# Constant matmuls at the start, later gates, paired merges and two GpSimd splits in a hybrid recurrent and attention layer

## The chip, the cores and the metric

The kernel runs on one core of one Trainium2 chip. A time is the device time of one execution in microseconds (us). Five engines work side by side, each on its own queue of instructions in program order: TensorE (PE in the views, PEld for its weight loads), VectorE (DVE), ScalarE (ACT), GpSimd (POOL) and SyncE (SP, which here issues most of the DMA transfers). An engine waits at an instruction until what the instruction needs has been signalled, and everything behind it on that queue waits too.

## The reference, cut to what matters

One layer of a streaming encoder, for 512 rows of a prompt and 8 x 16 rows of samples (640 rows, 5 tiles of 128), width 1024:

```python
z = rmsnorm(x) @ w_in                      # u, gate, q, k, v
r = sigmoid(blockdiag(xc, wa) + ba); ig = sigmoid(blockdiag(xc, wi) + bi)   # xc = conv(u)
lru = scan(exp(-8 * r * softplus(-lam)), sqrt(1 - a * a) * ig * xc) * gelu(gate)
attn = sink_softmax(band(q, k)) @ v        # 8 heads of 64, own chunk and two before
h = x + concat(rmsnorm(lru), rmsnorm(attn)) @ w_out
q = rmsnorm(h) @ w_query                   # 8 heads, two halves of 128
top16 of q1 @ keys1 and of q2 @ keys2, top16 of the 256 sums   # 16384 experts
y = h + sum(softmax(top) * gelu(u[idx] . rmsnorm(h)) * v[idx])
```

## The kernel before, in words

Every f32 matmul of weight is made of three: both operands are split into a high part (a copy in the type fp32r) and a low part (what is left), and high x high, high x low and low x high are summed in PSUM. A weight comes in slabs of 128x2048 f32: SyncE loads `raw`, ScalarE writes the high part `wh` (L95), VectorE or GpSimd writes the low part `wl` (L100), as the argument of `next_slab` or `put` says; both have two buffers.

The order in which the lines are written is the order on each engine. The stages by the trace: the projection of k and v on one eighth of the depth after another (0 to 43 us, L182, with x split by ScalarE and VectorE as it arrives, L193 and L194, weights at L197 and L198, and sums of squares on GpSimd, L204); the projections U, Q and G with the attention of the prompt and the gates of the recurrent part between them (to 160 us); the merges (to 250 us); turning the rows and the query (to 396 us) with VectorE's top-16 on each half (`query_keys`, L907 to L912, to 409 us); then the experts, computed densely: a loop over 64 slabs of U (389 to about 1090 us, L948) and one over 64 slabs of V (to 1741 us, L1335). A step of the U loop is two blocks of 24 matmuls, and each block reads all of the step's slab.

PSUM has two pools: `bank()` gives one of four one-bank buffers (name pb), `wide()` one of two two-bank buffers (name pa). A buffer is given again, in turn, when what read it last is done.

`project(s, n, between)` (L429) runs eight steps of six matmuls and calls one of `between` after each step. `lru_gates` (L381) gives eight such calls: a matmul of 128x332 into a bank (L393) and a sigmoid on ScalarE that reads it (L394). Ahead of the second call of `project(G0, ...)` stand scores of the attention (L468, L469), whose exponentials on ScalarE (L485) read four banks.

A merge (L622 to L631) is 12 matmuls of 128x512 into a bank: one tile of rows, one half of the width, of the recurrent or of the attention part. VectorE then reads it in one instruction: L635 adds it to the rows of x, L643 writes the sum to `h_rows`. There are ten of each: in order (half 0, tiles 0 to 4), (half 1, tiles 0 to 4), twice. I number them 1 to 20. Between the first ones other work of the attention lies on TensorE (L502, L510, L534, L560, L576), and calls of `next_slab(V)` stand behind merges 1, 5, 10 and 15. From merge 8 to merge 20 they follow one another.

In the U loop (L1261 on) `put` at L1273 splits the slab of the next step. At c=1 and c=2 VectorE's queue still holds the top-16 of the last query half ahead of these splits.

Of the kernel before, what the change touches and what calls it, by code (L numbers as in the profile page):

```python
# [16 lines left out]
P = 128  # L17
# [31 lines left out]
def hybrid_layer(ctx: ExitStack, tc: tile.TileContext, i, o):  # L49
    nc = tc.nc  # L50
    V, A, G, PE = nc.vector, nc.scalar, nc.gpsimd, nc.tensor
# [14 lines left out]
    def wide():  # L66
        return pss.tile([P, 2, 512], F32, name="pa", tag="pa", bufs=2)

    def bank():
        return pss.tile([P, 512], F32, name="pb", tag="pb", bufs=4)  # L70
# [12 lines left out]
    ones = const.tile([P, P], F32, name="ones")  # L83
# [9 lines left out]
    def high(raw):  # L93
        wh = stream.tile([P, 2048], F32R, name="wh", tag="wh")
        A.activation(wh, raw, AF.Copy)  # L95
        return wh

    def low(raw, wh, eng):
        wl = stream.tile([P, 2048], F32R, name="wl", tag="wl")
        eng.tensor_sub(wl, raw, wh.bitcast(F32))  # L100
        return wl

    def kc(w, c=256):
        return [x.rearrange("p (k c) -> p k c", c=c) for x in w]

    def proj_T(ps, w, xh, xl, c, ks=range(KD)):

        wh, wl = w
        cs = slice(c * P, (c + 1) * P)
        for k in ks:  # L110
            for n, (a, b) in enumerate(((wh, xh), (wh, xl), (wl, xh))):
                for hf in range(2):
                    PE.matmul(ps[:, hf, :H2], a[:, k, cs], b[:, k, hf * H2:(hf + 1) * H2],
                              start=(k == 0 and n == 0), stop=(k == KD - 1 and n == 2))
# [41 lines left out]
    def parts_tile():  # L156
        return (sh.tile([P, KD, T], F32R, name="xh", tag="xh"),
                sh.tile([P, KD, T], F32R, name="xl", tag="xl"))
# [8 lines left out]
    for r in (0, 64):  # L167
# [2 lines left out]
        G.memset(mask_q[r + 32:r + 33, 64:128].bitcast(F32), 1.0)  # L170
        G.memset(mask_k[r + 32:r + 33, 0:64].bitcast(F32), FAR)
    xh, xl = parts_tile()
    rs1 = Rstd(wk, D)
    kv_ps = [wide(), wide()]
    kv_ps = [kv_ps[t // 2][:, t % 2, :256] for t in range(4)] + [bank()[:, :256]]
# [205 lines left out]
    def lru_gates(pair):  # L381

        r2 = wk.tile([P, 3, UL], F32, name="rg2", tag="kcT")
        q2 = wk.tile([P, UL], F32, name="q2", tag="vc")
        r1_ = wk.tile([P, 2, D], F32, name="rg1", tag="rg1").rearrange("p a b -> p (a b)")
        q1 = wk.tile([P, UL], F32, name="q", tag="t640", bufs=3)
        rg[pair[0]] = (*[r1_[:, n * UL:(n + 1) * UL] for n in range(3)], q1)
        rg[pair[1]] = (*[r2[:, n] for n in range(3)], q2)

        def gate(ct, n, hf):  # L390
            pg = bank()[:, :XL // 2]
            part = slice(hf * (XL // 2), (hf + 1) * (XL // 2))
            PE.matmul(pg, gates[n][:, ct, :], xcs[ct][:, part], start=True, stop=True)  # L393
            A.activation(rg[ct][n][:, part], pg, AF.Sigmoid,  # L394
                         bias=small[("lru_ba", "lru_bi")[n]][:, ct:ct + 1])

        return [lambda ct=ct, n=n, hf=hf: gate(ct, n, hf) for ct in pair for n in range(2) for hf in range(2)]
# [31 lines left out]
    def project(s, n, between=()):  # L429
        ps = wide()  # L430
        for k in range(KD):
            proj_T(ps, kc(slabs[s]), xh, xl, n, (k,))
            if k < len(between):
                between[k]()
        return ps
# [170 lines left out]
    def rsqrt(dst, v, ps, t, n):  # L606

        V.tensor_scalar(v[:, t], ps, 1.0 / n, EPS, op0=ALU.mult, op1=ALU.add)
        G.tensor_tensor(dst[:, t], v[:, t], mhalf[:, t], ALU.pow)
# [6 lines left out]
    def attn_sum(t, sq):  # L616
# [2 lines left out]
            PE.matmul(ps, sq[:, k], ones[:, 0:1], start=(k == 0), stop=(k == CT - 1))  # L619
        rsqrt(ra, rv_a, ps, slice(t, t + 1), LW)  # L620

    def merge(s, t, k0):  # L622

        ps = bank()
        wh, wl = kc(slabs[s], 512)
        ts_ = slice(t * P, (t + 1) * P)
        for n, (a, b) in enumerate(((ch, wh), (ch, wl), (cl, wh))):
            for k in range(CT):
                PE.matmul(ps, a[:, k0 + k, ts_], b[:, k, :], start=(k == 0 and n == 0),
                          stop=(k == CT - 1 and n == 2))  # L630
        return ps  # L631
# [14 lines left out]
    A01, A23 = (0, 1), (2, 3)  # L646
    U0, U1, Q1, G0, G1, L0, _, A0 = range(1, 9)
# [44 lines left out]
    pg = project(G0, 0)  # L692
# [6 lines left out]
    a, b, c, d = pr[1]  # L699
# [1 line left out]
    a.softmax()  # L701
    gate_rows(0, pg)
    a.divide()
    pg = project(G0, 1, lru_gates(A23))

    exchange(a, b)
    gate_rows(1, pg)
# [5 lines left out]
    pg = project(G1, 0)  # L713
# [13 lines left out]
    pg = project(G1, 1)  # L727
# [186 lines left out]
    U = {}  # L914

    def u_load(c):
        U[c] = [load_slab(i["u"][c]), None, None]

    def put(table, c, eng):
        table[c][1] = high(table[c][0])  # L920
        table[c][2] = low(table[c][0], table[c][1], eng)
# [5 lines left out]
    for u in range(2, 2 * PH):  # L927
        c, n = u // 2, u % 2
        if n == 0 and c + 1 == PH:
            u_load(0)  # L930
        ps = wide()
# [252 lines left out]
    NS = NK // 2  # L1184
# [3 lines left out]
    used, c = 0.0, 2  # L1188
# [9 lines left out]
    def own_work(c):  # L1198

        nonlocal first  # L1200
        if first is None:
            if "selected" in keep:
                first = c + 1
            return
        n0, n1 = [min(NO, NO * (x - first) // (2 * NS - 2 - first)) for x in (c, c + 1)]
        for n in sorted(rows):
            consume(n)
            if n == NR - 1:
                own_acts()
        for n in range(n0, n1):  # L1210
            fetch(n)

    Pv = {}

    def v_load(c):
        Pv[c] = [load_slab(i["v"][2 * c:2 * c + 2].rearrange("j p d -> p j d")), None, None]
# [4 lines left out]
    def group_piece(g, q):  # L1221

        if g >= NG:
            return
        if q == 0:
            (pg, tg_), (pa, ta_) = (((p2, "gt"), (p2, "at")), ((sh, "xh"), (sh, "xl")))[g % 2]
            ga[g] = (pg.tile([P, NCH, JG, TG], F32, name="gt", tag=tg_),
                     pa.tile([P, JG, SD], F32, name="at", tag=ta_))
        gt, at = ga[g]
        n = NCH // 4  # L1230
        nc.sync.dma_start(gt[:, q * n:(q + 1) * n], Gd[g][:, q * n:(q + 1) * n])
        nc.sync.dma_start(at[:, 2 * q:2 * q + 2], Ad[g][:, 2 * q:2 * q + 2, :])
# [3 lines left out]
    def weigh(c):  # L1236

        gt, at = ga[2 * c // JG]
        j0 = 2 * c % JG
        W[c] = at[:, j0:j0 + 2]  # L1240
        av = W[c].rearrange("p j (c t) -> p j c t", t=TG)
        V.tensor_mul(av, av, gt[:, :, j0:j0 + 2, :].rearrange("p c j t -> p j c t"))  # L1242

    def weigh_split(c):
        a2 = W[c]
        ph = p2.tile([P, 2, SD], F32R, name="ph", tag="ph", bufs=2)
        A.activation(ph, a2, AF.Copy)  # L1247
        pl = p2.tile([P, 2, SD], F32R, name="pl", tag="pl", bufs=2)
        V.tensor_sub(pl, a2, ph.bitcast(F32))  # L1249
        W[c] = (ph, pl)  # L1250
# [4 lines left out]
    def gelu_out(c, n):  # L1255
        A.activation(act[c][:, n], u_ps[c, n][:, :SD], AF.Gelu_apprx_tanh)  # L1256
        if n == 1:
            jj = 2 * c % JG
            nc.sync.dma_start(Ad[2 * c // JG][:, jj:jj + 2, :], act[c])

    for c in range(NS):  # L1261
        if c + 2 < NS:
            u_load(c + 2)
        else:
            v_load(c + 2 - NS)
        if c in (NS - 3, NS - 2):
            for q in range(2):
                group_piece(0, 2 * (c - NS + 3) + q)
        act[c] = ap_.tile([P, 2, SD], F32, name="act", tag="act")
        if pending:  # L1270
            gelu_out(*pending)
        if c:
            put(*((U, c + 1) if c + 1 < NS else (Pv, 0)), V)  # L1273
        if c == NS - 1:
            weigh(0)
        own_work(c)
        placing = [p for p in (plan[c - 1] if c else []) if p[4]]
        for n in range(2):
            if c or n:
                u_block(c, n)  # L1280
            if n == 0:
                for p in placing[:2]:
                    if p[3]:
                        p[3]()
                for p in placing[:2]:
                    if p[3]:
                        p[4]()
                gelu_out(c, 0)
                for p in placing[:2]:
                    if not p[3]:  # L1290
                        p[4]()
            else:
                for p in placing[2:]:
                    if p[3]:
                        p[3]()
                    p[4]()
                pending = (c, 1)
        for p in plan[c]:
            p[2]()
        for p in plan[c + 1]:  # L1300
            if p[1]:
                p[1]()
        if p2 is None and c > 1 and not any(plan[c - 1:]):
            close_tb()
            close_ta()
            p2 = ctx.enter_context(tc.tile_pool(name="p2", bufs=1))
        if c == NS - 1:
            weigh_split(0)
            gelu_out(*pending)
# [131 lines left out]
```

## Time and profile before

| | us |
|---|---|
| median of three runs | 1734.81 |
| lowest and highest | 1734.61, 1750.63 |
| the profiled execution | 1743.01 |
| its span | 1741.2 |
| TensorE busy in it | 1686.4 (97%) |
| VectorE busy | 1415.8 (81%) |
| ScalarE, GpSimd busy | 680.5, 680.9 (39%) |

All times below come from the profiled execution, from its span's start. In a timeline row the first number is when an instruction, or a run of equal ones (xcount), began, the second how long it lasted; out<-in are the names of the tiles; in brackets stands how long the engine was idle before it and what it waited for. Matmuls overlap: the distance between two starts tells more than a duration. PEclk in a windows row is the granted clock, 1.00 being the upper of the two levels.

### The profile page before, as it was taken

The page shows a single profiled execution, that of the slowest core. Times are in us where ns is not written, and L with a number is a line of the kernel's source. Part 1 is how long each engine was busy: PE and PEld are TensorE (multiplying, and loading weights), DVE is VectorE, ACT ScalarE, POOL GpSimd, SP SyncE. Part 2 cuts the span into 40 slices and gives each one's busy share as a digit, 9 for nine tenths or more (in the row PEclk, how much of TensorE's full clock was granted, in tenths as well). Part 3 has the DMA queues.
Part 4 walks back from the last instruction along what each step waited for, and adds up shares of the span by engine and source line. Part 5 has one row for each costly group of instructions (what it writes and reads, how often), then busy time and mean ns, then how long its engine had stood idle before and what let it go on. Part 6 is the DMA issues. An engine that isn't in the chain of part 4 may idle for free.

```text
span 1741.2 us, 24849 instructions
## 1 busy us (share of the span) xinstructions
PE 1686.4 (97%) x9634; PEld 1546.6 (89%) x9634; DVE 1415.8 (81%) x2350; ACT 680.5 (39%) x790; POOL 680.9 (39%) x483
## 2 busy tenths in 40 slices
PE   8989999999999999999999999999999899999998
PEld 7887789998999898989899898899999799999997
DVE  7766565997667999988998895788888788888887
ACT  5457333223444445454455552332232223232222
POOL 4122003230101444443444444455555455555452
PEclk9999999999999999999999999999999999999999
DMA  5213233123546898999899999999999899999995
GB/s 167 101 50 109 75 103 94 69 73 139 207 180 211 303 389 282 370 346 351 301 377 370 374 379 398 396 376 377 378 390 378 339 381 388 379 371 392 380 351 221
DMA packets 180983, 492.67 MB, mean 283 GB/s; under 512 B 16817, under 2 KB 75057, under 8 KB 170225
## 3 DMA queue, kind: packets, MB, share of 16 engines
q1 hardware_dynamic: 125424, 289.73, 46.5%
q0 software_dynamic: 55296, 201.35, 30.2%
q8 instruction: 75, 1.23, 0.3%
q14 instruction: 44, 0.35, 0.1%
q10 hardware_dynamic: 144, 0.00, 0.0%
HBM read 426.11 MB, written 65.48 MB: 282 GB/s over the span
## 4 chain that ended last, share of the span: by engine, by line
DVE 30%; PE 19%; DMA 12%; issue 10%; ACT 4%; POOL 1%; ACTq 0%; DVEq 0%; POOLq 0%; SPq 0%
PE pa L948 13%; DVE wl L100 10%; DVE h_rows L1172 9%; DMA raw<-in_u 7%; PE po L1335 5%; DVE at L1242 3%; ACT ph L1247 3%; DVE h_rows L1167 2%; DVE ring L1167 2%; DMA raw<-in_v 2%; DMA gt<-Gd 2%; ACT wh L95 1%; PE pb L1122 1%; DVE oh L1110 1%; DMA Gd<-stage 1%
## 5 line engine op out<-in xcount | busy, mean ns | idle before, releaser
L100 DVE TENSOR_TENSOR wl<-raw,wh 128x2048 fp32r<-128x2048 f32 x137 | 313.2, 2287 | 107.2 <-ACT wh L95 104.0
L1335 PE MATMUL po<-ph,wh 128*128 128x448 f32 x1024 | 376.3, 367 | 11.3 <-ACT ph L1247 5.8
L948 PE MATMUL pa<-xh,wl 128*128 128x448 f32 x1024 | 375.3, 366 | 5.9 <-DVE wl L100 5.9
L1335 PE MATMUL po<-pl,wh 128*128 128x448 f32 x1024 | 377.4, 369 | 2.3 <-DVE pl L1249 2.2
L948 PE MATMUL pa<-xh,wh 128*128 128x448 f32 x1024 | 378.1, 369 | 0.0
L1335 PE MATMUL po<-ph,wl 128*128 128x448 f32 x1024 | 375.7, 367 | 0.0
L948 PE MATMUL pa<-xl,wh 128*128 128x448 f32 x1024 | 374.5, 366 | 0.0
L95 ACT ACTIVATE wh<-raw 128x2048 fp32r<-128x2048 f32 x146 | 279.5, 1915 | 192.9 <-PE po L1335 101.5
L1160 POOL DMA_INDIRECT h_rows<-in_u_rows,rowi x96 | 142.8, 1487 | 330.6 <-DVE h_rows L1167 239.1
L1335 PEld LDWEIGHTS po<-ph,wh 128*128 128x128 f32 x1024 | 193.4, 189 | 28.0 <-ACT ph L1247 6.2
L1335 PEld LDWEIGHTS po<-pl,wh 128*128 128x128 f32 x1024 | 193.3, 189 | 24.4 <-DVE pl L1249 7.8
L948 PEld LDWEIGHTS pa<-xh,wl 128*128 128x128 f32 x1024 | 192.9, 188 | 22.6 <-DVE wl L100 7.3
L1335 PEld LDWEIGHTS po<-ph,wl 128*128 128x128 f32 x1024 | 193.3, 189 | 15.5
L948 PEld LDWEIGHTS pa<-xl,wh 128*128 128x128 f32 x1024 | 193.1, 189 | 14.7
L948 PEld LDWEIGHTS pa<-xh,wh 128*128 128x128 f32 x1024 | 193.1, 189 | 14.7 <-ACT act L1256 0.2
L1160 POOL DMA_INDIRECT h_rows<-in_v,rowi x96 | 147.6, 1538 | 144.0 <-DVE h_rows L1172 121.0
L1160 POOL DMA_INDIRECT ring<-in_u_rows,rowi x96 | 142.4, 1484 | 143.7 <-DVE ring L1167 120.3
L1160 POOL DMA_INDIRECT ring<-in_v,rowi x96 | 148.2, 1544 | 121.4 <-DVE h_rows L1172 100.1
L1247 ACT ACTIVATE ph<-at 128x896 fp32r<-128x896 f32 x64 | 61.0, 953 | 339.4 <-DVE at L1242 339.4
L1256 ACT ACTIVATE act<-pa 128x448 f32<-128x448 f32 x128 | 71.6, 559 | 238.7 <-PE pa L948 169.3
L1130 ACT ACTIVATE stage<-pb 128x512 f32<-128x512 f32 x112 | 109.7, 1131 | 58.3 <-PE pb L1122 58.1
L1249 DVE TENSOR_TENSOR pl<-at,ph 128x896 fp32r<-128x896 f32 x64 | 69.9, 1092 | 73.0 <-ACT ph L1247 71.9
(270 smaller groups left out, 2483.7 us busy)
## 6 DMA issues: line engine op xcount, KB each, us to landing
raw<-in_u SPq DMA_DIRECT2D x64, 1024.0 KB
raw<-in_v SPq DMA_DIRECT2D x64, 1024.0 KB
Ad<-act SPq DMA_DIRECT2D x64, 448.0 KB
Gd<-stage SPq DMA_DIRECT2D x28, 1024.0 KB
gt<-Gd SPq DMA_DIRECT2D x64, 448.0 KB
at<-Ad SPq DMA_DIRECT2D x64, 448.0 KB
raw<-in_w_query SPq DMA_DIRECT2D x8, 1024.0 KB
raw<-in_w_out SPq DMA_DIRECT2D x4, 1024.0 KB
```

What stands on the lines that cost most here:

```text
L95: A.activation(wh, raw, AF.Copy)
L100: eng.tensor_sub(wl, raw, wh.bitcast(F32))
L948: PE.matmul(u_ps[c, n][:, :SD], a[:, k, n * P:(n + 1) * P], b[:, k, :SD], start=(k == 0 and m == 0), stop=(k == KD - 1 and m == 2))
L1130: A.activation(d["stage"][:, :, t0:t0 + 4].rearrange("p j t -> p t j"), d[n, f], AF.Copy, scale=1.0 / GSC)
L1160: G.indirect_dma_start(out=rows[n], out_offset=None, in_=table, in_offset=bass.IndirectOffsetOnAxis(ap=rowi[:, c:c + 1], axis=0))
L1167: V.scalar_tensor_tensor(row, row, 1.0, xrow[:, n // NS_], op0=ALU.mult, op1=ALU.mult, accum_out=dots[:, n:n + 1])
L1172: V.scalar_tensor_tensor(y, row, slots[:, c:c + 1], y, op0=ALU.mult, op1=ALU.add)
L1242: V.tensor_mul(av, av, gt[:, :, j0:j0 + 2, :].rearrange("p c j t -> p j c t"))
L1247: A.activation(ph, a2, AF.Copy)
L1249: V.tensor_sub(pl, a2, ph.bitcast(F32))
L1256: A.activation(act[c][:, n], u_ps[c, n][:, :SD], AF.Gelu_apprx_tanh)
L1335: PE.matmul(po[k][:, :SD], a[:, j, k * P:(k + 1) * P], b[:, j, :], start=(c == 0 and j == 0 and n == 0), stop=(c == NS - 1 and j == 1 and ...
```

## The change

It has four parts. Ten matmuls of the constant `ones` with itself go into a bank of their own at the start of TensorE's queue. The eight gates that lie between the steps of the second `project(G0, ...)` come three steps later, the last three behind the projection. A merge takes its bank from a two-bank buffer of `wide()`, which two merges in a row share. And the low parts of the slabs 2 and 3 of U are made by GpSimd.

```diff
--- before.py
+++ after.py
@@ -170,6 +170,10 @@
         G.memset(mask_q[r + 32:r + 33, 64:128].bitcast(F32), 1.0)
         G.memset(mask_k[r + 32:r + 33, 0:64].bitcast(F32), FAR)
     xh, xl = parts_tile()
+
+    idle_ps = bank()
+    for _ in range(10):
+        PE.matmul(idle_ps[:, :P], ones, ones, start=True, stop=True)
     rs1 = Rstd(wk, D)
     kv_ps = [wide(), wide()]
     kv_ps = [kv_ps[t // 2][:, t % 2, :256] for t in range(4)] + [bank()[:, :256]]
@@ -619,9 +623,14 @@
             PE.matmul(ps, sq[:, k], ones[:, 0:1], start=(k == 0), stop=(k == CT - 1))
         rsqrt(ra, rv_a, ps, slice(t, t + 1), LW)
 
+    merge_ps = []
+
     def merge(s, t, k0):
 
-        ps = bank()
+        if not merge_ps:
+            two_banks = wide()
+            merge_ps.extend([two_banks[:, 1], two_banks[:, 0]])
+        ps = merge_ps.pop()
         wh, wl = kc(slabs[s], 512)
         ts_ = slice(t * P, (t + 1) * P)
         for n, (a, b) in enumerate(((ch, wh), (ch, wl), (cl, wh))):
@@ -701,7 +710,10 @@
     a.softmax()
     gate_rows(0, pg)
     a.divide()
-    pg = project(G0, 1, lru_gates(A23))
+    late = lru_gates(A23)
+    pg = project(G0, 1, [lambda: None] * 3 + late[:5])
+    for gate in late[5:]:
+        gate()
 
     exchange(a, b)
     gate_rows(1, pg)
@@ -1270,7 +1282,7 @@
         if pending:
             gelu_out(*pending)
         if c:
-            put(*((U, c + 1) if c + 1 < NS else (Pv, 0)), V)
+            put(*((U, c + 1) if c + 1 < NS else (Pv, 0)), G if c <= 2 else V)
         if c == NS - 1:
             weigh(0)
         own_work(c)
```

The rows of the order that follow are instructions in program order on one engine: the line, the operation, out<-in, the shape and, in brackets, the signals that this instruction waits for (DVE is VectorE's, Activation ScalarE's, PE TensorE's own). Lines of the changed kernel are 4 to 12 higher: L397 is the gate (L393 before), L638 the merge (L629 before).

First, TensorE in the second `project(G0, ...)`. Before, from its first step:

```order
L113 MATMUL pa<-xh,wh 128x320 x2
L113 MATMUL pa<-xl,wh 128x320 x2
L113 MATMUL pa<-xh,wl 128x320 x2
L393 MATMUL pb<-xc,wa 128x332 [waits PE_49]
L113 MATMUL pa<-xh,wh 128x320 x2
L113 MATMUL pa<-xl,wh 128x320 x2
L113 MATMUL pa<-xh,wl 128x320 x2
L393 MATMUL pb<-xc,wa 128x332 [waits Activation_49]
```

In the change, the end of the third step on:

```order
L113 MATMUL pa<-xh,wh 128x320 x2
L113 MATMUL pa<-xl,wh 128x320 x2
L113 MATMUL pa<-xh,wl 128x320 x2
L113 MATMUL pa<-xh,wh 128x320 x2
L113 MATMUL pa<-xl,wh 128x320 x2
L113 MATMUL pa<-xh,wl 128x320 x2
L397 MATMUL pb<-xc,wa 128x332 [waits PE_49]
L113 MATMUL pa<-xh,wh 128x320 x2
L113 MATMUL pa<-xl,wh 128x320 x2
L113 MATMUL pa<-xh,wl 128x320 x2
L397 MATMUL pb<-xc,wa 128x332 [waits Activation_49]
```

The first gate stands behind the fourth step, and its waits are as before: the third and the fourth wait for VectorE and ScalarE, which read the scores' banks.

Second, TensorE at merges 10 to 12. Before:

```order
L629 MATMUL pb<-wh,xh 128x512 [waits DVE_49]
L629 MATMUL pb<-wh,xh 128x512 x3
L629 MATMUL pb<-wl,xh 128x512 x4
L629 MATMUL pb<-wh,xl 128x512 x4
L629 MATMUL pb<-wh,xh 128x512 [waits DVE_49,Activation_49]
L629 MATMUL pb<-wh,xh 128x512 [waits Activation_49] x3
L629 MATMUL pb<-wl,xh 128x512 x4
L629 MATMUL pb<-wh,xl 128x512 x4
L629 MATMUL pb<-wh,xh 128x512 [waits DVE_49]
L629 MATMUL pb<-wh,xh 128x512 x3
L629 MATMUL pb<-wl,xh 128x512 x4
L629 MATMUL pb<-wh,xl 128x512 x4
```

In the change, from merge 10 (its first row has the wait) over merge 11 (its `x4` wait only for ScalarE, which makes their input) to merge 12:

```order
L638 MATMUL pa<-wh,xh 128x512 [waits DVE_49]
L638 MATMUL pa<-wh,xh 128x512 x3
L638 MATMUL pa<-wl,xh 128x512 x4
L638 MATMUL pa<-wh,xl 128x512 x4
L638 MATMUL pa<-wh,xh 128x512 [waits Activation_49] x4
L638 MATMUL pa<-wl,xh 128x512 x4
L638 MATMUL pa<-wh,xl 128x512 x4
L638 MATMUL pa<-wh,xh 128x512 [waits DVE_49]
L638 MATMUL pa<-wh,xh 128x512 x3
L638 MATMUL pa<-wl,xh 128x512 x4
L638 MATMUL pa<-wh,xl 128x512 x4
```

Before, the wait of merge 12 is for VectorE's read of merge 8, whose bank it takes over. In the change it is for VectorE's read (L652, which is L643 before) of merge 11, the first half of the same buffer. All second merges of a pair (2, 4, 6 and so on to 20) have such a wait, each for VectorE's read (L644 or L652) of the merge right before; the first ones have none for it.

Third, GpSimd's queue at the start of the U loop. Before:

```order
L958 IOTA first_of 128x128
L961 IOTA column 128x256
L964 IOTA io_4053 128x256
L1160 DMA h_rows<-in_u_rows,rowi 128x1024 [waits DVE_49]
L1160 DMA h_rows<-in_u_rows,rowi 128x1024
```

In the change:

```order
L970 IOTA first_of 128x128
L973 IOTA column 128x256
L976 IOTA io_4054 128x256
L100 TENSOR_TENSOR wl<-raw,wh 128x2048 [waits DMAHW4_49,PE_49,Activation_49]
L100 TENSOR_TENSOR wl<-raw,wh 128x2048 [waits DMAHW5_49,PE_49,Activation_49]
L1172 DMA h_rows<-in_u_rows,rowi 128x1024 [waits DVE_49]
```

Two splits (L100) stand between the last iota and the first gather (L1172, which is L1160 before). Nothing else moved on this queue, and VectorE's has two splits less.

## Rows read from the trace of the kernel before

**Rows 1.** Profile page, part 1: engine, busy us (share of the span) x instructions

```profile
PE 1686.4 (97%) x9634; PEld 1546.6 (89%) x9634; DVE 1415.8 (81%) x2350; ACT 680.5 (39%) x790; POOL 680.9 (39%) x483
```

**Rows 2.** Waits of TensorE, whole span: line, line waited for, us, times, longest

```profile
PE pb L1122 <- DVE ow L1114: 9.7, 7, 2.1
```

**Rows 3.** Timeline of TensorE, start; columns: start us, us, instruction, idle before

```profile
5.90 0.58 PE L182 MATMUL pa<-wh,xh 128*128 128x256 f32 x1 [5.90 <-ACT wh L197]
...
18.41 0.39 PE L182 MATMUL pa<-wl,xh 128*128 128x256 f32 x1 [1.56 <-DVE wl L198]
```

**Rows 4.** Timeline of VectorE, same stretch

```profile
1.41 0.17 DVE L84 MEMSET ones<- 128x128 f32 x1
...
5.93 0.69 DVE L198 TENSOR_TENSOR wl<-raw,wh 128x512 fp32r<-128x512 f32 x1
...
10.14 2.04 DVE L198 TENSOR_TENSOR wl<-raw,wh 128x512 fp32r<-128x512 f32 x1
```

**Rows 5.** Timeline of GpSimd, same stretch

```profile
9.83 3.78 POOL L204 TENSOR_TENSOR sq<-sq 128x640 f32<-128x640 f32 x2 [0.29 <-ACT sq L202]
```

**Rows 6.** Timeline of TensorE, second gate projection

```profile
118.96 0.56 PE L113 MATMUL pa<-xh,wh 128*128 128x320 f32 x2
...
119.95 0.72 PE L393 MATMUL pb<-xc,wa 128*128 128x332 f32 x2
...
121.39 0.72 PE L393 MATMUL pb<-xc,wa 128*128 128x332 f32 x2
...
126.61 0.83 PE L393 MATMUL pb<-xc,wi 128*128 128x332 f32 x2 [3.62 <-ACT p L485]
...
136.05 0.60 PE L502 MATMUL pb<-ident,p 128*128 128x128 f32 x4
```

**Rows 7.** Windows: busy us of PE, PEld, DVE, ACT, POOL; granted clock; DMA share; GB/s

```profile
128.00:129.00 1.00, 1.00 (x5) 1.00 (x4) 0.13 (x1) 0.99 (x3) 0.00 (x0) 0.50 0.00 0
179.00:181.00 2.00, 2.00 (x6) 1.53 (x5) 0.00 (x0) 2.00 (x9) 0.77 (x1) 0.50 0.00 0
```

**Rows 8.** Timeline of TensorE, merges

```profile
178.57 1.98 PE L629 MATMUL pb<-wh,xh 128*128 128x512 f32 x4 [1.33 <-DVE rv L136]
...
183.03 1.04 PE L502 MATMUL pb<-ident,p 128*128 128x128 f32 x8
...
204.38 1.17 PE L629 MATMUL pb<-wh,xh 128*128 128x512 f32 x4
...
220.64 1.07 PE L629 MATMUL pb<-wh,xh 128*128 128x512 f32 x4
...
226.08 1.07 PE L629 MATMUL pb<-wh,xh 128*128 128x512 f32 x4
```

**Rows 9.** Timeline of VectorE, same stretch

```profile
184.27 1.41 DVE L635 SCALAR_TENSOR_TENSOR rows<-pb,rr,rows 128x512 f32<-128x512 f32 x2
...
207.94 0.74 DVE L635 SCALAR_TENSOR_TENSOR rows<-pb,rr,rows 128x512 f32<-128x512 f32 x1
...
220.84 0.75 DVE L635 SCALAR_TENSOR_TENSOR rows<-pb,rr,rows 128x512 f32<-128x512 f32 x1 [0.92 <-PE pb L629]
...
227.72 0.75 DVE L643 SCALAR_TENSOR_TENSOR h_rows<-pb,ra,rows 128x512 f32<-128x512 f32 x1
```

**Rows 10.** Timeline of TensorE, second step of the U loop

```profile
411.36 0.74 PE L948 MATMUL pa<-xh,wl 128*128 128x448 f32 x1 [4.31 <-DVE wl L100]
...
414.59 0.36 PE L948 MATMUL pa<-xh,wl 128*128 128x448 f32 x1
...
415.81 0.36 PE L948 MATMUL pa<-xh,wl 128*128 128x448 f32 x1
```

**Rows 11.** Timeline of ScalarE, same stretch

```profile
397.40 1.91 ACT L95 ACTIVATE wh<-raw 128x2048 fp32r<-128x2048 f32 x1
...
407.12 1.90 ACT L95 ACTIVATE wh<-raw 128x2048 fp32r<-128x2048 f32 x1
```

**Rows 12.** Instructions of line 100: count, duration ns min/median/max, first and last start

```profile
L100 POOL TENSOR_TENSOR wl<-raw,wh x9: 4613/4628/4649, 265.3 to 388.1; 128x2048 fp32r<-128x2048 f32 x9
```

## The prediction

> **What bounds the kernel now.** I read the page first: TensorE is busy for 97% of the span [rows 1], so a change moves the time only by what it takes out of, or puts into, TensorE's row of work. Then the waits of TensorE over the whole span: the largest group is 9.7 us in seven pieces in the late loops [rows 2], which no edit touches; what the edits touch lies in four short places ahead of 412 us. For these I read the timeline of TensorE to see when it stands, then that of the engine it stands for. The reader is to see the idle time in brackets at the right end of a row: 5.90 and 1.56 us at the start [rows 3], 3.62 us at the third gate [rows 6], 1.33 us at the second merge [rows 8], 4.31 us at the split of slab 2 of U [rows 10]. [...]
>
> Behind 412 us nothing moves against its neighbours: every loop step is issued behind the one before, and TensorE is the engine with least slack. So I pass each shift of TensorE on to the end whole.
>
> **The change, part by part.**
>
> *Matmuls on constants.* Ten 128x128 products of a constant in f32. The smallest rows of that size are eight transposes in 1.04 us, 0.13 each [rows 8]; such an f32 product shows as two instructions in this trace, so 20 x 0.13 = 2.6 us, or 5.2 us at the low clock. They wait for the memset of the ones, done at 1.58 [rows 4], and end at 4.2 or at 6.8, against a first projection matmul at 5.90 [rows 3]. What they may bring is a faster projection. But that projection stands still again until 18.41 for VectorE's low part of a weight piece [rows 3], and VectorE's chain there waits for loads, ScalarE and itself, not for TensorE. So a quicker start only lengthens the 1.56 us stand, and a start 0.9 us late only shortens it. Upper end of the gain: nothing excludes that a few tenths pass; upper end of the loss: one fall of the clock at 18.41, where the stand is longer, 1.7 us by the price worked out under the merges. I take **0**.
>
> *Gates three steps later.* One step and its gate take 1.44 us (119.95 to 121.39), a step alone 0.99 at most (118.96 to 119.95) [rows 6]. The third gate is ready at 126.61 - 3.62 = 122.99 and stands for a PSUM bank that ScalarE's exponentials still read. Three plain steps ahead of it make it ready at 125.6 to 126.0; the exponentials do not depend on it, so 0.6 to 1.0 us of the stand is left and 2.6 to 3.0 go. From 119.95 to 136.05 are 16.1 us; less seven rounds of 1.44, a last gate of some 0.5 and the stand, 1.9 us is left, which is what the clock at 0.50 costs [rows 6, 7]. A stand of 1 us should not bring that fall: TensorE's 0.2 to 0.3 us are given back where the last three gates, now back to back, follow ScalarE's sigmoids. Gain 2.6 + 1.9 - 0.2 = **4.3 us**; 2.4 if the clock falls all the same.
>
> *Merges in pairs in a two-bank tile.* This is the term that decides. The twenty merges are each 2.72 us of TensorE (220.64 to 226.08 is two) [rows 8] and stood in banks of a ring of four, so that a merge rarely met VectorE. Now two merges share one tile. In the order of the change (the second place shown) the first matmul of every second merge carries a wait for VectorE, and the program fulfils it with VectorE's read of the first half of the same tile: the dependence is kept by tile, not by bank. So the second merge of a pair cannot start while the first is being read. What is late is read off VectorE's rows:
> - Merge 2: the read of merge 1 stands behind a slab split and starts at 184.27; two reads take 1.41, one 0.70. Start 184.97 instead of 178.57 [rows 8, 9]: +6.4 (the 1.33 us stand is inside it).
> - Merge 4: attention work lies between the halves: 0. Merge 8, in the same way: +0.1.
> - Merge 6: the read of merge 5 is behind a split too, 207.94 + 0.74 = 208.68 against 204.38: +4.3.
> - Merge 12: 227.72 + 0.75 = 228.47 against 226.08: +2.4.
> - Merges 10, 14, 16, 18, 20: back to back with their first halves. Read at 220.84 for 0.75, so 221.59 against 220.64 [rows 8, 9]: +0.95 each, 4.8.
>
> Sum 18.0. Behind each waiting merge all of TensorE's queue stands, and VectorE, which reads each merge as soon as it can, has no backlog in which the delay could vanish. Merge 2 ran at the low clock and took 183.03 - 178.57 = 4.46 instead of 2.72 [rows 7, 8]: a fall costs a merge 1.7. It stays at that price; merge 6 now follows 4.3 us of idle, as the matmuls after 4.31 us of idle in the U loop and after 3.62 us at the gate did when the clock fell, so +1.7. Together **+19.7**. Lower bound: 0 (the halves independent). Upper bound: a fall at every wait, six more, 10.4.
>
> [...] The row first: the stands that brought 0.50 are the long ones, or the 1.33 us one after light work. [...]
>
> *Two splits of U on GpSimd.* Before, both stand behind VectorE's top-k and TensorE gets slab 2 at 411.36, 4.31 us late, then runs at the low clock: 9 matmuls in 3.23 us, where six take 1.22 right after [rows 10], so 3.23 - 1.83 = 1.4 lost. On GpSimd a split takes 4.63 (nine of them, 4.61 to 4.65) [rows 12]. ScalarE's high part of slab 2 is there at 397.40 + 1.91 = 399.3 [rows 11]: ready at 403.9, needed at 411.36 - 4.31 = 407.05. Slab 3: 407.12 + 1.90 + 4.63 = 413.7, needed a step of 48 matmuls after slab 2, 48 x 0.203 = 9.7 us, at 416.8. GpSimd has nothing else then. Gain 4.3 + 1.4 = **5.7**. Moved past: only the gathers come behind these splits on GpSimd's queue, and those wait for indices that VectorE works out after its top-k. VectorE is rid of two splits while it is late. Lower bound: the third rival.
>
> **Sum**: 0 - 4.3 + 19.7 - 5.7 = +9.7 us. The profiled execution took 1743.01, so 1752.7 on its terms; it lies 8.2 over the median shown, 1734.81, and against that median I forecast **1744.5**, 0.56% slower. A measurement of this kernel tells about 1% from no change: 17.3 us, so 1717.5 to 1752.2 counts as the same.
>
> **Rivals.**
> 1. *The halves are independent*: the edit gives each merge a bank, and no more. Then the merge term is 0 to -1.3 and the others stay: -10.0 to -11.3, **1724**. For it: the two halves are different banks. [...] Against it: the wait in the order. It decides whether a second merge starts before VectorE's first read. 5%.
> 2. *The clock falls at the short waits too*: up to 6 x 1.74 = 10.4 more, **1755**, slower by more than 1%; it takes five of six falls. For it: merge 2's stand of 1.33 us was enough. Against it: the stands between are 0.95 us, and merges keep TensorE full in between. 10%. Merge 12 alone would give 1746.
> 3. *GpSimd's splits are stretched by VectorE.* VectorE's own subtract went from 0.69 to 2.04 us beside GpSimd's adds [rows 4, 5]. Three times 4.63 is 13.9: slab 2 at 413.2, 6.1 late, and slab 3 some 4 more, so +4 to +6 in place of -5.7: **1755**. It decides when a split passes 7.7 us (407.05 - 399.3). Against it: nine splits beside the same top-k at 4.61 to 4.65. 3%.
> 4. *Later waits swallow part of it*: the late loops wait for VectorE and loads at 9.7 us in all, and work that runs ahead of TensorE could be earlier by the shift: **1736**. Against it: those waits are in the step of the loops, not in an absolute time. 6%.
>
> My forecast keeps 76%. Its own bounds: 1738 (no fall at merge 6, a quicker start, a little less per wait) to 1750 (gates still at the low clock, a loss at the start, merge 12 at the low clock). With rival 4 and most of rival 2 the range is **1735 to 1754**. Faster by over 1%: 2%, slower by over 1%: 12% (rivals 2 and 3), within: 86%.
>
> **What would show it.** In the changed profile TensorE's first merge matmuls must show waits for VectorE's reads of merge results, ten at most, some 18 us in all beside the clock, longest at merges 2 and 6; the gate's wait near 1 us and no 0.50 at 128; no stand at 407 for the split; the projection at the start still going on at 18.4. I would be wrong if second merges start with no wait, if the clock shows 0.50 through the later merges, or if the GpSimd splits take over 7 us.

## The result and the profile after

The changed kernel took 1753.32 us (median of 21 runs, 1748.08 to 1756.63), the kernel before 1739.6 (21 runs, 1730.24 to 1750.63; the 1734.81 of the forecast was the median of its first three). The ratio is 1.0077, 95% interval 1.0062 to 1.0091: 13.4 us slower, 10.8 to 15.8. The forecast was 9.7 us slower on the median then known, with 1735 to 1754 as its range: the time lies inside it, near its upper end, and in the class it gave 86%, within 1%. Laid on 1739.6 instead, the same range would be 1740 to 1759.

The waits of TensorE in the changed kernel's profile, over the whole span (us in total, times, longest):

```profile
PE pa L638 <- DVE rows L644: 12.5, 3, 7.5
PE pa L638 <- DVE h_rows L652: 5.9, 5, 2.3
PE po L1347 <- ACT act L1268: 5.2, 1, 5.2
PE pb L1134 <- DVE ow L1126: 4.4, 5, 2.1
...
PE pb L397 <- ACT p L489: 1.0, 1, 1.0
```

The first two rows are new: eight stands of a merge for VectorE's read of a merge, 18.4 us. No row for a slab split (L100) is left, and the gate's wait is 1.0 instead of 3.62 [rows 6].

The timeline of TensorE at the merges, with the first transposes of the rows (L836) behind merge 20:

```profile
162.75 0.50 PE L638 MATMUL pa<-wh,xh 128*128 128x512 f32 x1 [1.59 <-ACT xh L752]
...
181.45 2.08 PE L638 MATMUL pa<-wh,xh 128*128 128x512 f32 x4 [7.53 <-DVE rows L644]
...
186.44 1.03 PE L506 MATMUL pb<-ident,p 128*128 128x128 f32 x8
...
212.13 1.20 PE L638 MATMUL pa<-wh,xh 128*128 128x512 f32 x4 [4.11 <-DVE rows L644]
...
221.02 2.07 PE L638 MATMUL pa<-wh,xh 128*128 128x512 f32 x4
...
232.69 1.20 PE L638 MATMUL pa<-wh,xh 128*128 128x512 f32 x4 [0.84 <-DVE rows L644]
...
240.73 2.07 PE L638 MATMUL pa<-wh,xh 128*128 128x512 f32 x4 [2.28 <-DVE h_rows L652]
...
245.14 1.09 PE L638 MATMUL pa<-wh,xh 128*128 128x512 f32 x4
...
271.74 1.91 PE L836 MATMUL pb<-ident,xn 128*128 128x128 f32 x16
```

These are merges 1, 2, 6, 7, 10, 12 and 13; they answer to [rows 8]. In the kernel before, merge 1 and the first transposes are these rows:

```profile
166.36 0.50 PE L629 MATMUL pb<-wh,xh 128*128 128x512 f32 x1 [1.59 <-ACT xh L740]
...
250.57 1.91 PE L824 MATMUL pb<-ident,xn 128*128 128x128 f32 x16
```

Merge 1 starts 3.6 us earlier than before, the transposes 21.17 us later: 24.8 us were lost between. VectorE, at the reads those stands were for:

```profile
178.44 2.29 DVE L100 TENSOR_TENSOR wl<-raw,wh 128x2048 fp32r<-128x2048 f32 x1 [3.54 <-ACT wh L95]
180.65 0.74 DVE L644 SCALAR_TENSOR_TENSOR rows<-pa,rr,rows 128x512 f32<-128x512 f32 x1
...
211.33 0.74 DVE L644 SCALAR_TENSOR_TENSOR rows<-pa,rr,rows 128x512 f32<-128x512 f32 x1
...
239.93 0.74 DVE L652 SCALAR_TENSOR_TENSOR h_rows<-pa,ra,rows 128x512 f32<-128x512 f32 x1
```

Read a row of one against the other: the read ends at 181.39 and merge 2 starts at 181.45; 212.07 and 212.13; 240.67 and 240.73. Each time 0.06 us lie between. And the windows (columns as in [rows 7]):

```profile
129.00:131.00 2.00, 2.00 (x11) 1.63 (x10) 0.00 (x0) 1.78 (x4) 0.07 (x1) 1.00 0.00 0
182.00:185.00 3.00, 3.00 (x8) 2.31 (x7) 0.00 (x0) 0.00 (x0) 0.00 (x0) 0.50 0.86 333
214.00:216.00 2.00, 2.00 (x7) 1.48 (x5) 0.00 (x0) 0.00 (x0) 0.00 (x0) 0.50 0.77 324
222.00:224.00 2.00, 2.00 (x7) 1.58 (x6) 1.05 (x3) 1.65 (x3) 0.00 (x0) 0.60 0.82 275
241.00:243.00 2.00, 2.00 (x5) 1.54 (x6) 0.00 (x0) 0.00 (x0) 0.00 (x0) 0.50 0.89 283
256.00:258.00 2.00, 2.00 (x10) 1.65 (x9) 1.28 (x1) 0.69 (x1) 0.00 (x0) 1.00 0.00 0
```

No 0.50 at the gates any more; 0.50 at merges 2, 6, 7 and 12 (0.60 is the end of that of merge 7); 1.00 at merge 16, which stood for 1.01 us. The clock is also at 0.50 at merges 1 and 5 (167 to 170 and 204 to 206 us), as in the kernel before (0.50 from 169 to 170 and from 200 to 202).

### The profile page after: what moved, and what is told of

It reads as the page before. It is cut to its first block, busy times and chain, and to the rows that moved or that the text cites. A ratio compares the mean times of both kernels' runs of the same rounds, so it can differ in the third digit from the quotient of the medians.

```text
span 1751.6 us, 24885 instructions
## 1 busy us (share of the span) xinstructions
PE 1695.5 (97%) x9654; PEld 1551.0 (89%) x9654; DVE 1415.8 (81%) x2348; ACT 680.1 (39%) x790; POOL 683.4 (39%) x485
## 4 chain that ended last, share of the span: by engine, by line
PE 46%; DVE 31%; DMA 8%; issue 8%; ACT 6%; POOL 0%; ACTq 0%; DVEq 0%; SPq 0%
PE pa L960 22%; DVE wl L100 9%; DVE h_rows L1184 9%; PE pa L113 8%; PE po L1347 5%; PE pa L638 3%; DVE at L1254 3%; ACT ph L1259 3%; DMA raw<-in_u 2%; DVE ring L1179 2%; DMA raw<-in_v 2%; PE pb L1134 2%; DMA gt<-Gd 2%; DVE h_rows L1179 2%; PE pb L186 1%
## 5 line engine op out<-in xcount | busy, mean ns | idle before, releaser
L100 DVE TENSOR_TENSOR wl<-raw,wh 128x2048 fp32r<-128x2048 f32 x135 | 308.7, 2286 | 98.1 <-ACT wh L95 94.9
L1172 POOL DMA_INDIRECT h_rows<-in_u_rows,rowi x96 | 142.3, 1482 | 303.8 <-DVE h_rows L1179 236.8
L1172 POOL DMA_INDIRECT h_rows<-in_v,rowi x96 | 147.6, 1537 | 144.1 <-DVE h_rows L1184 121.1
L1172 POOL DMA_INDIRECT ring<-in_v,rowi x96 | 148.1, 1543 | 121.6 <-DVE h_rows L1184 100.3
L1172 POOL DMA_INDIRECT ring<-in_u_rows,rowi x96 | 136.6, 1423 | 147.3 <-DVE ring L1179 124.2
```

The costliest lines, as they stand in the source:

```text
L1172: G.indirect_dma_start(out=rows[n], out_offset=None, in_=table, in_offset=bass.IndirectOffsetOnAxis(ap=rowi[:, c:c + 1], axis=0))
```

## The experiments

Ten more kernels ran, each timed in 5 to 12 executions beside 11 to 29 of the kernel before. The table has what was measured; the us are the ratio's, on the median of the kernel before beside it; "transposes" is the start of the first transposes of the rows in the run's profile.

| run | ratio to before (95%) | us against before | transposes, us |
|---|---|---|---|
| the change | 1.0077 (1.0062, 1.0091) | +13.4 | 271.74 |
| x1_bank_merges | 0.9924 (0.9902, 0.9946) | -13.2 | 248.97 |
| x2_merges_only | 1.0138 (1.0114, 1.0163) | +24.0 | 276.90 |
| x3_alternate | 0.9932 (0.9908, 0.9955) | -11.8 | 247.28 |
| x4_gates_splits | 0.9933 (0.9908, 0.9957) | -11.6 | 249.23 |
| x5_warm_only | 0.9999 (0.9983, 1.0015) | -0.2 | 253.10 |
| x6_gates_only | 0.9972 (0.9958, 0.9986) | -4.9 | 247.82 |
| x7_splits_only | 0.9954 (0.9936, 0.9971) | -8.0 | 252.09 |
| x10_read_first | 1.0002 (0.9987, 1.0016) | +0.3 | 257.52 |
| x11_alt_read_first | 0.9933 (0.9911, 0.9954) | -11.7 | 245.31 |
| x12_bank_read_first | 0.9937 (0.9910, 0.9963) | -11.0 | 249.32 |

**x1_bank_merges**, the change less the pairs:

```diff
-        if not merge_ps:
-            two_banks = wide()
-            merge_ps.extend([two_banks[:, 1], two_banks[:, 0]])
-        ps = merge_ps.pop()
+        ps = bank()
```

> The change with one part undone: merges take one-bank buffers again. Theory (the dependence is kept by two-bank tile, so every second merge waits for VectorE's read of the first): no wait of a merge for the read of the merge before it, the first transposes of the rows (250.57 us in the kernel before, 271.74 in the change) at 246.3 to 247.0, none of the clock's falls at merges 6, 7 and 12, and a time 9 to 10 us below the kernel before. Rival (the loss sits in another part: the constant matmuls, the gates or the GpSimd splits): the transposes stay behind 255 us, or the time stays above the kernel before.

One part taken out turns +13.4 into -13.2 us (-17.0 to -9.4; 9 to 10 were expected). No merge waits for the read before it; the one stand of merge 2 is the old one, for L136 (1.33 us). The transposes came 2 us later than the theory said: single merge matmuls took up to 0.80 us there against a median of 0.39, as in the kernel before, where the clock is at 0.50 at merges 1, 2 and 5, and those stretches differ from run to run (see the last section). The rival falls.

**x2_merges_only**, the same part alone in the kernel before:

```diff
-        ps = bank()
+        if not merge_ps:
+            two_banks = wide()
+            merge_ps.extend([two_banks[:, 1], two_banks[:, 0]])
+        ps = merge_ps.pop()
```

> The paired merges alone, in the kernel before. Theory: merge 2 starts 6.4 us late, merge 6 another 4.3, merge 12 another 2.4, the other pairs about 1 each, and the clock falls at merges 6, 7 and 12; the transposes of the rows at 275.4 (24.8 us later than before), and the time 22 to 26 us longer. By the forecast as it was written the merges cost 19.7 us: transposes at 270.3. Rival (halves independent, the loss is elsewhere): transposes at 249 to 251, the time as before.

Slower by 24.0 us (19.8 to 28.3), transposes 26.3 us later. Its waits in the stretch of the merges are those of the change, so this is a price of the pairs and not of their meeting with the other parts:

```profile
PE pa L634 <- DVE rows L640: 12.8, 3, 7.8
PE pa L634 <- DVE h_rows L648: 5.9, 5, 2.3
```

**x3_alternate** keeps both halves of a two-bank buffer in use, but deals them so that neighbours do not share:

```diff
-            two_banks = wide()
-            merge_ps.extend([two_banks[:, 1], two_banks[:, 0]])
+            x, y = wide(), wide()
+            merge_ps.extend([y[:, 1], x[:, 1], y[:, 0], x[:, 0]])
```

> The change with the same two-bank buffers dealt out otherwise: two buffers are taken at once and four merges in a row go to the first half of one, the first half of the other, then the second halves. A merge then shares its buffer with the merge two before it. Theory: VectorE's read of that one is over by the time, so the waits of merges 2, 6, 10 to 20 go, transposes of the rows at 246.3 to 247.5, time 9 to 10 us below the kernel before. Rival (a ring of two two-bank buffers is too short for twenty merges, whoever shares): waits for reads stay, transposes at 255 us or later, time at or above the kernel before.

11.8 us faster than before. Same buffers, same number of merges in each; of 18.4 us of waits one of 1.35 is left, merge 3 for the read of merge 1, which now shares its tile:

```profile
PE pa L638 <- DVE rows L644: 1.3, 1, 1.3
```

So the ring of two is not too short. What costs is that the next merge is the one that shares, which tells the dependence by tile apart from a reason that lies in the number of buffers.

**x10_read_first** leaves the pairs as in the change and moves what the reads stood behind. The slab splits at merges 1, 5 and 11 go behind VectorE's reads:

```diff
-    next_slab(V)
     merge_lru_out(0, 0, ps0)
+    next_slab(V)
...
-    next_slab(V)
     merge_lru(0, 4)
+    next_slab(V)
...
     merge_lru(1, 4)
-    next_slab(V)
...
         merge_attn(0, t)
+        if t == 0:
+            next_slab(V)
```

> The change, with three slab splits moved behind VectorE's reads of merges 1, 5 and 11, which they stood ahead of; the pairs still share a tile. Theory: the wait of a second merge is exactly the time until VectorE has read the first, so merge 2 waits some 4.4 us less than in the change, merge 6 not at all, merge 12 about 1 us in place of 2.3, and the falls of the clock at merges 6, 7 and 12, which follow those waits, go too: first transposes of the rows at 255 to 262 in place of 271.7, time 10 to 15 us below the change and within 5 us of the kernel before. Rival (the waits are set by something else in the pairs, or the falls come whatever the waits are): transposes at 266 us or later.

Merges 2, 6, 10 and 12, and the windows over merges 7 to 20, in its profile:

```profile
177.13 2.08 PE L638 MATMUL pa<-wh,xh 128*128 128x512 f32 x4 [2.29 <-DVE rows L644]
...
203.87 1.21 PE L638 MATMUL pa<-wh,xh 128*128 128x512 f32 x4
...
221.45 1.20 PE L638 MATMUL pa<-wh,xh 128*128 128x512 f32 x4 [0.84 <-DVE rows L644]
...
228.05 1.20 PE L638 MATMUL pa<-wh,xh 128*128 128x512 f32 x4 [0.84 <-DVE h_rows L652]
```

```profile
206.00:256.00 50.00, 44.65 (x207) 34.35 (x206) 25.31 (x37) 12.69 (x19) 2.16 (x4) 1.00 0.34 112
```

The stand of merge 2 went from 7.53 to 2.29 us, that of merge 6 is gone, that of merge 12 went from 2.28 to 0.84, and the clock is 1.00 from merge 7 on: 13 us better than the change by the two ratios, from the order of three instructions on VectorE. The pairs are still worse by 11 to 14 us than one bank each (x1, x4 and x12). The profiles of x10 and x1 differ by 9.8 us; 8.2 of these lie between merge 1 and the transposes (95.0 us against 86.8 in x1), at merge 2 and at the six later stands of 0.84 to 1.00 us.

**x4_gates_splits**: both other parts alone, no constant matmuls. **x5_warm_only**, **x6_gates_only**, **x7_splits_only**: one part each in the kernel before. Their edits are the pieces of the change's diff.

> Gates three steps later and the two GpSimd splits alone: no constant matmuls, merges as before. Theory: gates -4.3 us, splits -5.7 us, together 10 us below the kernel before, and within 0.7 us of the run with the constant matmuls and one-bank merges, since those matmuls bring nothing. Rival (the constant matmuls are worth 1 to 3 us by an earlier warm clock): this run 1 to 3 us above that one, its projection of k and v ending later.

> The ten constant matmuls alone, in the kernel before. Theory: the projection of k and v waits for VectorE's low parts and for loads in either case, so it ends within 0.7 us of the kernel before and the time is the same within 1 us. Rival (an earlier high clock is worth its 2.7 us): the second gate projection, at 118.96 us before, starts at 116 to 117 and the time is 2 to 3 us shorter.

> The gates three steps later alone, in the kernel before. Theory: the wait of the third gate goes from 3.62 to about 1.0 us, no 0.50 of the clock at 127 to 131, the first merge starts 4.2 us earlier, and the time is 3 to 5 us shorter. Rival (the gain is given back at the merges, where the clock falls in other places): the first merge is 4 us earlier but the first transposes of the rows only 1 to 2 us, as in the two runs with gates, splits and one-bank merges.

> The two splits on GpSimd alone, in the kernel before. Theory: GpSimd takes 4.6 us for each, the wait of 4.31 us for the split of slab 2 and the low clock behind it go, time 5 to 6 us shorter. Rival (GpSimd is stretched by VectorE beside it): splits of 6 us or more and part of the wait left; or the late loops give the gain back: time the same.

x4 and x1 differ by the constant matmuls alone: 0.9933 and 0.9924. x4 is 1.6 us the slower, as its rival said, but the intervals overlap widely, and the sign that the rival named is missing: the projection of k and v has its last matmul at 42.39 in x4 and at 42.40 in x1. x5 is 0.2 us from before (-3.0 to +2.6), and its second gate projection starts at 119.34, not at 116 to 117. The matmuls bring nothing that can be measured. The rows say why. With them the projection's first matmuls do run closer together, 0.12 us from start to start from 7.3 us on in all five profiles that have them; in the seven without them it is 0.21 until 9.6 to 12.1 us. (The granted clock reads 1.00 there in both kinds, so it does not show what makes the difference.) But what is gained so goes into a stand for VectorE that comes ahead of the one at 18.4 [rows 3], as in x5:

```profile
12.62 0.39 PE L186 MATMUL pa<-wl,xh 128*128 128x256 f32 x1 [1.56 <-DVE wl L202]
...
18.78 0.39 PE L186 MATMUL pa<-wl,xh 128*128 128x256 f32 x1 [1.56 <-DVE wl L202]
```

Gates: -4.9 us (-7.3 to -2.4). In x6 the first merge starts 43.14 us behind the first step of that projection, where it was 47.40: 4.26 us, and the time agrees. Splits: -8.0 us (-11.1 to -5.0), where 5 to 6 were expected; no stand for slab 2, and no stretching, over all eleven of GpSimd's splits in that run:

```profile
L100 POOL TENSOR_TENSOR wl<-raw,wh x11: 4605/4631/4645, 266.9 to 410.6; 128x2048 fp32r<-128x2048 f32 x11
```

**x11_alt_read_first** puts x3's dealing and x10's order together, without the constant matmuls; **x12_bank_read_first** is x4 with x10's order.

> A version meant to keep what helped: gates three steps later, the two GpSimd splits, two-bank buffers dealt out to four merges in turn, VectorE's reads of merges 1, 5 and 11 ahead of the slab splits, no constant matmuls. Theory: no merge waits for a read, the 1.33 us at merge 2 or 3 goes too, time 10 to 13 us below the kernel before. Rival (nothing is left there beyond what the gates and splits gave): the same time within 1.5 us as with gates and splits alone.

> As the gates and splits alone, with one-bank merges, and with VectorE's reads of merges 1, 5 and 11 ahead of the slab splits. Theory: in a ring of four banks no merge stood for those reads, so the order of reads and splits is worth nothing here: time within 1.5 us of gates and splits alone, 10 to 11 us below the kernel before. Rival (late reads hold up the ring of four as well): 2 us or more below gates and splits alone.

x1, x3, x4, x11 and x12 are all 11 to 13 us faster than the kernel before; their intervals overlap, so none is told apart from the others. So what x11 adds to x4 cannot be measured, as its rival said, though its way from merge 1 to the transposes is the shortest of all (82.7 us). In x12 the order of reads and splits brings nothing that can be measured (-11.0 us against x4's -11.6) where a merge does not share with the next one. All five beat both kernels; the simplest is x4: gates and splits, merges in a ring of four.

## Why the prediction was right, step by step

The direction and the mechanism held: by x1, x2 and x3 it is the guard on a whole tile that makes the change slower, and every other part is a gain or nothing. The size of one term was too small, and the gain of another part was too small as well, which hid half of that: that the sum came within 4 us is partly luck.

- **Constant matmuls, 0.** Held (x5). They took 4.17 us, between the 2.6 and 5.2 of the forecast. The projection resumed at 18.90 instead of 18.41 [rows 3], because its first weight piece was there 0.5 us later (ScalarE, after its load, at 5.70 instead of 5.22); the second gate projection starts at 118.96 to 120.48 in the profiles without these matmuls and at 119.00 to 119.62 in those with them, so it is no effect of theirs. That the stand at 18.4 for VectorE stays was right: 1.56 us in both. A quicker start did not lengthen it, though; it brought a second stand of 1.56 ahead of it, at 12.73 in the change.
- **Gates, -4.3.** -4.27 in the profile (162.75 - 119.62 = 43.13 against 166.36 - 118.96 = 47.40), -4.9 timed alone. The wait left was 0.97, and the clock did not fall: 1.00 from 119 to 136 us.
- **Merges, +19.7.** 24.8 in the profile, 24.0 timed alone: the step that was mis-sized. Of the 24.8 the later starts at the waits, each against the start of the merge ahead, make 18.6, against 18.0 forecast: merge 2 6.5 (6.4), merge 6 4.3 (4.3), merge 12 2.45 (2.4), and 1.0 to 1.2 for merges 10, 14, 16, 18 and 20 (0.95). The clock makes 5.5, against 1.7: 1.9 at merge 6 (1.7), but also 0.5 more at merge 2, 1.4 at merge 7 and 1.7 at merge 12 (245.14 - 240.73 = 4.41 instead of 2.72). The last 0.7 are 0.15 us at which each merge behind a stand runs slower, which the forecast left out. It priced merge 12's fall only as an upper bound; both profiles that have its stand of 2.28 us (the change and x2) show the fall, 0.50 from 241 to 243 and from 248 to 250 us; the kernel before, x5, x6, x7, x10, x11 and x12, without that stand, are at 1.00 there.
- **Splits, -5.7.** Right in place, and timed alone -8.0, whose interval holds 5.7. The U loop, first to last matmul, is 690.7 to 700.1 us long in the four profiles with VectorE's splits and 682.5 to 687.3 in the eight with GpSimd's; the 4.31 and 1.4 us of the forecast are the part that was named, and all four have it and none of the eight. The rest of the difference lies mostly in other waits and other falls of the clock: less TensorE's waits in the loop (2.4 to 15.6 us) and less half of its time at 0.50 (0 to 5.1 us, an estimate: in the kernel before, the loop's matmuls start 0.37 us apart at 0.50, from 411.90 on, and 0.20 at 1.00), the loop takes 679.1 to 682.6 us in all twelve. The waits for `ow` are 9.7 us in the kernel before and 4.4 in the change, but 2.4 in x6, which has VectorE's splits. Whether the splits on GpSimd shorten any of this is not shown.

The rivals: *independent halves* fell to the rows at merges 2, 6 and 12, which start 0.06 us behind VectorE's reads. *The clock falls at the short waits too* fell in its own form: behind none of the stands of 0.84 to 1.01 us is the clock at 0.50, in the change or x10; but part of its price came in by merge 12. What the prediction held for it, that merge 2's stand of 1.33 us was enough for a fall, was no sign of it: merge 2 ran at 0.50 in x5, x6 and x11 too, after stands of 0.32, 0.26 and none. Short idles between groups, six of them of 0.84 to 1.00 us one behind the other in x10, left the clock at 1.00 for 50 us. *GpSimd stretched* fell: 4.61 to 4.65 us. *Later waits swallow part*: not shown. In the two profiles the difference at the end is 10.4 us, less than 21.2 at the first U block less 5.7 for the splits; but the kernel before has 5.3 us more of waits for `ow`, which differ as much between profiles with the same splits (9.7 there, 2.4 in x6). By the ratio the kernels differ by 13.4 us, and 21.2 less the 8.0 that the splits gave alone is 13.2.

## What to carry to other kernels

Before two accumulations share one on-chip buffer of two banks, look at what the program waits for: if the guard is by tile, the second cannot start until the first has been read, and the price is the whole delay of that read on its engine's queue, not the 0.75 us of the read (merge 2 stood for 7.53 us). One way out costs nothing that can be measured: let a buffer be shared by work that is not adjacent (x3). Another takes back half: put the read ahead of long work on the reader's queue (x10, 13 us better than the change and still 11 to 14 behind one bank each). And a part that makes things worse can hide parts that help: each was worth timing alone, and dropping the pairs gives 11 to 13 us over the kernel before.

## What the runs showed of the hardware that was not expected

The clock falls in the merges' stretch in every run, at partly different places, and at some of them without any wait: windows of ten profiles show 0.50 there, and in x1 and x3 single merge matmuls took 0.80 us against a median of 0.39. In the kernel before, merge 5 has 0.50 from 200 to 202 us and no stand ahead of it. In x4 merge 7 ran at 0.50 although TensorE stood for nothing there; it came behind eight pairs of small products (128 and 16 rows of weights, 64 columns). The window over its end, in x4's profile:

```profile
206.00:212.00 6.00, 6.00 (x20) 4.56 (x20) 1.90 (x5) 2.89 (x5) 0.00 (x0) 0.50 0.61 223
```

x11 and x12 show a fall at merge 7 too (0.50 from 206 to 208 and from 206 to 212 us); x5, x6, x7, x10 and the kernel before do not (1.00). The change and x2, the two with merge 6's stand, both do (0.60 from 222 to 224, 0.50 from 224 to 228). So the 1.4 us at merge 7 in the change need not come from merge 6's stand, and the stretch from merge 1 to the transposes differs by up to 3 us between runs that have no new wait there: 84.2 us in the kernel before and x7, 84.7 in x6, 86.8 in x1, 87.1 in x4 and x12. One profile's position is good to about that, which is why the ratios of many runs, not the positions, decide between versions here.
